# Turned feed-forward rows copied out of PSUM first and split from the copy, the last product of w_down in banks of its own, and the last row divided at column 352

## Chip, cores and metric

The kernel runs on one core of a Trainium2 chip, as one launch. The metric is the device time of the launch in microseconds (us), smaller is better. Engines are named as in the profile: PE is TensorE (matrix products and transposes), PEld its weight loads, DVE is VectorE, ACT is ScalarE, POOL is GpSimd, SP is SyncE, which issues most DMAs. The granted TensorE clock of the profiled execution is 0.999 of full speed.

## What is computed

The reference is one encoder layer on 512 tokens of width 1024 in float32. Two mixers (a state-space scan and a gated MLP) are merged and added to the residual stream `h`, a cross-attention to 256 memory tokens follows, then a gated feed-forward block, then a last normalization. The change lies in the last two:

```python
def rms_norm(x, g):
    xf = x.astype(jnp.float32)
    y = xf * lax.rsqrt(jnp.mean(xf * xf, axis=-1, keepdims=True) + EPS)
    return (y * g.astype(jnp.float32)).astype(x.dtype)

def swiglu(hn, w_gate, w_up, w_down):
    return (jax.nn.silu(hn @ w_gate) * (hn @ w_up)) @ w_down
...
        h = h + memory_cross_attention(rms_norm(h, xattn_norm_g[i]), memn,
                                       w_q[i], w_k[i], w_v[i], w_xo[i])
        h = h + swiglu(rms_norm(h, ffn_norm_g[i]), w_gate[i], w_up[i], w_down[i])
    return rms_norm(h, final_norm_g)
```

`w_gate` and `w_up` are 1024 by 2816, `w_down` is 2816 by 1024.

## The kernel before

**Numbers in two halves.** Every large product keeps float32 accuracy by splitting each operand into a high half (`hi`, the value rounded by ScalarE to the type that TensorE multiplies, L85) and a low half (`lo`, the value minus `hi`, a DVE subtraction, L86). A product is three matmuls, hi by hi, hi by lo and lo by hi (`mm3`, L374). Weights come by DMA into `wraw` (three buffers) and are split into `whi` and `wlo` (three buffers each) some steps ahead of their use; a fixed list, `plan`, gives the order of loads and splits, and `next_w` moves along it.

**Rows.** The 512 tokens are four rows of 128 tokens, numbered 0 to 3. The residual stream `h` holds each row as 128 partitions by 1024 columns, and its column halves are `HALF[0]` and `HALF[1]`.

**Turned rows.** The feed-forward products need the normalized rows with features on the partitions. Once a row of `h` is final, its sum of squares is taken (L500), GpSimd takes the root (L511), DVE scales the row into `xs` (two halves, L526), and `to_feat` turns it: for each half `q`, four transposes on TensorE write one PSUM buffer `ptr` (L534), then `split` makes `fn_hi` (ScalarE) and `fn_lo` (DVE) from it, and ScalarE copies it unsplit into `full` (L540). `ptr` comes from the pool `paux`, which has three buffers. `full` is needed since the gate and up products run in Strassen form: sums of quarters of the activation are made from it (L1720 to L1730). Rows 0 and 1 are turned between the blocks of the attention's output product, in written order; rows 2 and 3 among the first feed-forward products (`pf`, `px`, `pv`), where the scheduler places them.

**The product with w_down.** It is a Strassen product of seven (`DOWN`, in the order 1, 5, 2, 6, 3, 7, 4), each of six chunks of rows of `w_down`; chunk 5 is half as deep as the others. A product covers two rows of tokens and 512 columns. Its partial results lie in pairs of PSUM banks `dx`, `dv` and `dq` and are added into `h` by DVE (`onto_h`, L1934). Products 6, 7 and 4 accumulate on top of each other in `dx`, and `h` takes what is there after 6 and after 7. Product 4 is the last: it is needed only for rows 2 and 3, second half. Its first three chunks run for both rows, the last three (`HELD`) first for row 2 and then, in two pieces of 256 columns in `dv`, for row 3, seeded with the sum of `h` and the bank (L1902).

**The end.** Each row's first finished half is multiplied by the gain `g_o` early and kept in `hg`, a part of the tile `rest` (L1874). When a row's second half is done, its sum of squares gives the factor `r` (L1880, L1881), `hg` is scaled by ScalarE (L1918), the other half by DVE (L1920, L1926, L1928), and both are stored. For row 3 SyncE stores the part of `hg` and ScalarE's queue the part of `h`. From the last chunk's products on, the order of DVE and ACT is the written one (`in_order`).

Of the kernel before, what the change touches and what calls it, by code (L numbers as in the profile page):

```python
# [11 lines left out]
AF = mybir.ActivationFunctionType  # L12
ALU = mybir.AluOpType
# [4 lines left out]
P = 128  # L18
D = 1024
T = 512  # L20
NT = T // P
# [31 lines left out]
def hybrid_layer_kernel(  # L53
# [8 lines left out]
    nc = tc.nc  # L62
    x, mem, out = x[0], mem[0], out[0]
# [13 lines left out]
    def bank(name):  # L77
        return pm.tile([P, 512], F32, tag="mm", name=name)

    def aux(name, shape=(P, 512)):  # L80
        return pa.tile(list(shape), F32, tag="aux", name=name)

    def split(dst_hi, dst_lo, src):

        hi = nc.scalar.copy(dst_hi, src)  # L85
        lo = nc.vector.tensor_tensor(dst_lo, src, dst_hi.bitcast(F32), ALU.subtract)  # L86
        if pinned[0]:
            in_order(hi)
            in_order(lo)
        return hi  # L90
# [3 lines left out]
    in_order = tc.keep_in_program_order  # L94
# [165 lines left out]
    DOWN, CHUNKS = (1, 5, 2, 6, 3, 7, 4), 6  # L260
# [110 lines left out]
    def mm3(ps, a, b, start, stop, free=False, turn=False):  # L371

        for i, (x, y) in enumerate(((0, 0), (0, 1), (1, 0))):
            m = nc.tensor.matmul(ps, a[x], b[y], start=start and i == 0, stop=stop and i == 2, skip_group_check=free)  # L374
            if turn:
                in_order(m)
# [90 lines left out]
    def tick(us=5.2):  # L467

        side["now"] += us / 5.2
        run_due()  # L470
        side["credit"] = min(side["credit"] + us * side["rate"], us)
        while side["credit"] > 0.0 and side["gen"] is not None:
            try:
                used = next(side["gen"])
            except StopIteration:
                side["gen"] = None
                return
            if used is None:
                side["credit"] = 0.0
                return  # L480
            side["credit"] -= used
# [32 lines left out]
    HALF = (slice(0, 512), slice(512, 1024))  # L514
# [10 lines left out]
        for i in range(2):  # L525
            nc.vector.scalar_tensor_tensor(dst[:, HALF[i]], src[:, HALF[i]], r, g[:, HALF[i]], ALU.mult, ALU.mult)  # L526

    def to_feat(src, hi, lo, tsl, full=None, skip=None, part=(0, 1), turned=False):

        for q in part:  # L530
            ps = aux("ptr", (P, 4, P))
            for j in range(4):
                k = 4 * q + j
                m = nc.tensor.transpose(ps[:, j, :], src[:, k * P:(k + 1) * P], ident)  # L534
                if turned:
                    in_order(m)
            if q != skip:
                split(hi[:, 4 * q:4 * q + 4, tsl], lo[:, 4 * q:4 * q + 4, tsl], ps)
            if full is not None:
                nc.scalar.copy(full[:, 4 * q:4 * q + 4, tsl], ps)  # L540

    xsp = [None]
# [11 lines left out]
    def slot(tag, shape, dt, name, place=NEAR):  # L554
        n = math.prod(shape[1:])
        t = sp.tile([P, KD * T + ROOM[tag]], dt, tag=tag, name=name)[:, place[tag]:place[tag] + n]
        return t.rearrange("p (a b c) -> p a b c", a=shape[1], b=shape[2]) if len(shape) == 4 else (
            t.rearrange("p (a b) -> p a b", a=shape[1]))

    def token_slot(name, place=NEAR):  # L560
        return tuple(slot(tag, (P, KD, T), F32R, name, place) for tag in "BC")
# [374 lines left out]
    turned = set()  # L936
# [263 lines left out]
    for h in range(H):  # L1200
        ps = bank("psv")
# [56 lines left out]
    def unit_bank(name):  # L1258
        return bank(name).rearrange("p (j t) -> p j t", j=2)
# [15 lines left out]
    part = slot("A", (P, KD, T), F32, "part")  # L1275
# [133 lines left out]
    h = slot("A", (P, NT, D), F32, "h")  # L1409
# [202 lines left out]
    fn_hi, fn_lo = token_slot("fn", AWAY)  # L1612
# [3 lines left out]
    ps = {t: bank(f"pt{t}") for t in range(NT)}  # L1616
# [32 lines left out]
    full = fp.tile([P, KD, T], F32, tag="full", name="full", bufs=1)  # L1649


    scaled = {}
# [3 lines left out]
        rms_scale(h[:, t, :], g_f, xs, ss)  # L1656

    def turn_row(t, turned=False):
        to_feat(scaled.pop(t), fn_hi, fn_lo, slice(t * P, (t + 1) * P), full, turned=turned)

    fin = add_evac(1, 1, scale_row)
    held, ps = [], {}
# [91 lines left out]
    ps = [bank("pf0"), bank("pf1")]  # L1754
# [51 lines left out]
    def rows_product(ps, q, c, ops_, ts, cs, start, stop, turn=False):  # L1806
        hi, lo = ops_
        a = made[q, c // 2]
        for t in ts:
            tsl = slice(t * P, (t + 1) * P)  # L1810
            for k in range(hi.shape[1]):
                kk = 2 * (c % 2) + k
                mm3(ps[t], (a[0][:, kk, tsl], a[1][:, kk, tsl]), (hi[:, k, cs], lo[:, k, cs]),
                    start and k == 0, stop and k == hi.shape[1] - 1, True, turn)
        tick(1.35 * len(ts))
# [6 lines left out]
    for i, u in enumerate(UNITS):  # L1822
        final = i == len(UNITS) - 1
        x, v = begun
        q = unit_bank("pq")
# [12 lines left out]
        else:  # L1838
            dx = [bank(f"dx{t}") for t in range(2)]
# [20 lines left out]

    g_o = gain(final_norm_g, "g_o")
    hg = rest[0][:, 4:8, :]
    msq = fp.tile([P, NT + 2], F32, name="msq", bufs=1)

    def mean_sq(dst, ss, base):
# [2 lines left out]
    early, HELD = {}, 3  # L1868

    def first_half(t, half):  # L1870

        early[t] = half
        sum_sq(hss[:, 2, t, half:half + 1], h[:, t, HALF[half]])
        nc.vector.tensor_tensor(hg[:, t, :], h[:, t, HALF[half]], g_o[:, HALF[half]], ALU.mult)  # L1874
        nc.vector.tensor_scalar(msq[:, t:t + 1], hss[:, 2, t, half:half + 1], 1.0 / D, EPS, ALU.mult, ALU.add)

    def inv_root(t, ss):
        r = np_.tile([P, 1], F32, tag="r", name="r", bufs=2)
        ms = np_.tile([P, 1], F32, tag="ms", name="ms", bufs=2)
        root = nc.scalar.activation(ms, ss, AF.Sqrt, bias=msq[:, t:t + 1], scale=1.0 / D)  # L1880
        inv = nc.vector.reciprocal(r, ms)  # L1881
        if pinned[0]:
            in_order(root)
            in_order(inv)
        return r
# [11 lines left out]
    last = [dv[i][:, 0:256] for i in range(2)]  # L1897
    last_cols = [slice(512 + 256 * i, 768 + 256 * i) for i in range(2)]

    def seed_last(ps):  # L1900
        for i in range(2):
            in_order(nc.vector.tensor_tensor(last[i], h[:, NT - 1, last_cols[i]], ps[:, 256 * i:256 * i + 256], ALU.add))  # L1902

    def finish_last(i):
        ss = np_.tile([P, 2], F32, tag="ss", name="ss", bufs=2)
        sum_sq(ss[:, 0:1], last[i])
        in_order(nc.vector.tensor_tensor(h[:, NT - 1, last_cols[i]], last[i], g_o[:, last_cols[i]], ALU.mult))
        if i == 0:
            mean_sq(msq[:, NT:NT + 1], ss[:, 0:1], msq[:, NT - 1:NT])
        else:  # L1910
            write(NT - 1, inv_root(NT, ss[:, 0:1]))

    stores = []

    def write(t, r):
        rows = out[t * P:(t + 1) * P]
        cs, hs = HALF[early[t]], HALF[1 - early[t]]
        scaled = nc.scalar.activation(hg[:, t, :], hg[:, t, :], AF.Copy, scale=r)  # L1918
        if t < 2:
            nc.vector.scalar_tensor_tensor(h[:, t, hs], h[:, t, hs], r, g_o[:, hs], ALU.mult, ALU.mult)  # L1920
            stores.extend([(rows[:, cs], hg[:, t, :]), (rows[:, hs], h[:, t, hs])])
            return
        in_order(scaled)
        nc.sync.dma_start(rows[:, cs], hg[:, t, :])
        if t == NT - 1:
            in_order(nc.vector.tensor_scalar(h[:, t, hs], h[:, t, hs], r, None, ALU.mult))  # L1926
        else:
            in_order(nc.vector.scalar_tensor_tensor(h[:, t, hs], h[:, t, hs], r, g_o[:, hs], ALU.mult, ALU.mult))  # L1928
        (nc.scalar if t == NT - 1 else nc.sync).dma_start(rows[:, hs], h[:, t, hs])

    def onto_h(ps, t0, half, op):
        for t in range(2):
            hs = h[:, t0 + t, HALF[half]]
            nc.vector.tensor_tensor(hs, hs, ps[t], op)  # L1934

    dq = [bank("dq0"), aux("dq1")]
# [7 lines left out]
    for t in range(2):  # L1944
        first_half(t, 1)
# [5 lines left out]
        finish(t)  # L1951
    down_product(dx, 7, False)
    onto_h(dx, 2, 0, ALU.subtract)
    for t in range(2, 4):
        first_half(t, 0)

    held = []
    for c in range(CHUNKS):
        ops_ = next_w(w_down, 4, c)
        if c == CHUNKS - 1 - LOADS:  # L1960
            for dst, src in stores:
                in_order(nc.sync.dma_start(dst, src))
        if c < CHUNKS - HELD:
            rows_product(dx, 4, c, ops_, (0, 1), slice(0, 512), False, c == CHUNKS - HELD - 1)
        else:
            held.append((c, ops_))
    seed_last(dx[1])
    for c, ops_ in held:
        rows_product(dx, 4, c, ops_, (0,), slice(0, 512), False, c == CHUNKS - 1, True)
    pinned[0] = True  # L1970
    in_order(nc.vector.tensor_tensor(h[:, 2, HALF[1]], h[:, 2, HALF[1]], dx[0], ALU.add))
    finish(2)
    for i in range(2):
        for c, ops_ in held:
# [36 lines left out]
```

## Time and profile before

| | us |
|---|---|
| median of 3 runs | 864.61 (863.97 to 865.8) |
| profiled execution, its own time | 865.88 |
| its span | 864.1 |
| PE busy | 855.3 (99%) |
| DVE busy | 662.2 (77%) |
| ACT busy | 465.9 (54%) |
| POOL busy | 88.4 (10%) |

The span is the part of the profiled execution between its first and last instruction. A line of the groups or of the timeline names the source line, the engine, the operation, what it writes and reads with shapes, its count, and in brackets how long its engine was idle ahead of it and what ended that idle time. All moments are microseconds from the start of the span.

### The profile page before, as it was taken

The page shows a single profiled execution, that of the slowest core. Times are in us where ns is not written, and L with a number is a line of the kernel's source. Part 1 is how long each engine was busy: PE and PEld are TensorE (multiplying, and loading weights), DVE is VectorE, ACT ScalarE, POOL GpSimd, SP SyncE. Part 2 cuts the span into 40 slices and gives each one's busy share as a digit, 9 for nine tenths or more (in the row PEclk, how much of TensorE's full clock was granted, in tenths as well). Part 3 has the DMA queues.
Part 4 walks back from the last instruction along what each step waited for, and adds up shares of the span by engine and source line. Part 5 has one row for each costly group of instructions (what it writes and reads, how often), then busy time and mean ns, then how long its engine had stood idle before and what let it go on. Part 6 is the DMA issues. An engine that isn't in the chain of part 4 may idle for free.

```text
span 864.1 us, 14763 instructions
## 1 busy us (share of the span) xinstructions
PE 855.3 (99%) x5776; PEld 766.1 (89%) x5776; DVE 662.2 (77%) x1077; ACT 465.9 (54%) x698; POOL 88.4 (10%) x119
## 2 busy tenths in 40 slices
PE   9999999999999999999999999999999999999997
PEld 7888888888889988899899887999999999988886
DVE  7698999899646867678758655867877768899875
ACT  6734863244445544457557544645545454655674
POOL 0002211211021110010010001001211111000000
PEclk9999999999999999999999999999999999999999
DMA  8759576988574798635696455557899898366664
GB/s 271 191 166 315 100 216 157 234 201 208 139 220 157 248 308 267 218 112 197 214 273 169 130 160 134 146 167 182 207 241 231 213 229 219 96 192 205 199 187 155
DMA packets 116041, 170.09 MB, mean 197 GB/s; under 512 B 9458, under 2 KB 80642, under 8 KB 115843
## 3 DMA queue, kind: packets, MB, share of 16 engines
q1 hardware_dynamic: 95618, 140.07, 49.3%
q0 software_dynamic: 20064, 28.55, 20.4%
q8 instruction: 45, 0.74, 0.3%
q10 hardware_dynamic: 288, 0.52, 0.2%
q14 instruction: 26, 0.21, 0.1%
HBM read 160.23 MB, written 48.73 MB: 242 GB/s over the span
## 4 chain that ended last, share of the span: by engine, by line
PE 96%; DVE 1%; DMA 1%; issue 0%; ACT 0%; POOL 0%; SPq 0%; POOLq 0%; ACTq 0%
PE pf L374 27%; PE pt L374 15%; PE px L1250 13%; PE dx L374 7%; PE pq L1250 6%; PE dq L374 3%; PE pv L1250 3%; PE bx L1250 3%; PE qx L1250 3%; PE dv L374 2%; PE pz L958 2%; PE qv L1250 1%; PE po L374 1%; PE psc L374 1%; PE py L1014 1%; PE qq L1250 1%
## 5 line engine op out<-in xcount | busy, mean ns | idle before, releaser
L85 ACT CAST whi<-wraw 128x1024 fp32r<-128x1024 f32 x141 | 145.3, 1030 | 163.9 <-PE pf L374 56.3
L86 DVE TENSOR_TENSOR wlo<-wraw,whi 128x1024 fp32r<-128x1024 f32 x141 | 168.4, 1196 | 59.7 <-ACT whi L85 58.9
L374 PE MATMUL pf<-xn,whi 128*128 128x512 f32 x448 | 139.6, 392 | 0.0
L374 PEld LDWEIGHTS pf<-xn,whi 128*128 128x128 f32 x448 | 83.5, 188 | 16.7
L374 PE MATMUL pf<-xn,wlo 128*128 128x512 f32 x224 | 87.8, 392 | 0.0
L1250 PE MATMUL px<-fn,whi 128*128 128x256 f32 x480 | 83.4, 277 | 0.0
L1250 PEld LDWEIGHTS px<-fn,whi 128*128 128x128 f32 x480 | 72.5, 188 | 0.2
L86 DVE TENSOR_TENSOR wlo<-b,whi 128x1024 fp32r<-128x1024 f32 x40 | 49.0, 1224 | 26.0 <-ACT whi L85 26.0
L85 ACT CAST whi<-b 128x1024 fp32r<-128x1024 f32 x40 | 42.2, 1054 | 48.7 <-PE px L1250 27.8
L1250 PE MATMUL px<-fn,wlo 128*128 128x256 f32 x240 | 66.4, 277 | 0.0
L1250 PE MATMUL pq<-s,whi 128*128 128x256 f32 x320 | 55.0, 276 | 0.0
L374 PE MATMUL dx<-whi,s 128*128 128x512 f32 x166 | 52.2, 391 | 0.4 <-DVE h L1934 0.4
L86 DVE TENSOR_TENSOR wlo<-t,whi 128x1024 fp32r<-128x1024 f32 x30 | 36.7, 1225 | 18.4 <-ACT whi L85 18.4
L85 ACT CAST whi<-t 128x1024 fp32r<-128x1024 f32 x30 | 31.6, 1054 | 34.2 <-PE pv L1250 11.4
L374 PEld LDWEIGHTS pf<-xn,wlo 128*128 128x128 f32 x224 | 42.0, 188 | 8.9 <-issue 0.2
L1250 PEld LDWEIGHTS pq<-s,whi 128*128 128x128 f32 x320 | 48.2, 188 | 0.0
L1250 PEld LDWEIGHTS px<-fn,wlo 128*128 128x128 f32 x240 | 45.1, 188 | 0.0
L1250 PE MATMUL pq<-s,wlo 128*128 128x256 f32 x160 | 44.2, 276 | 0.0
L374 PE MATMUL pt<-whi,xn 128*128 128x512 f32 x128 | 43.1, 403 | 0.0
L374 PEld LDWEIGHTS dx<-whi,s 128*128 128x128 f32 x166 | 31.1, 188 | 7.4 <-ACT whi L85 0.8
L374 PE MATMUL dx<-wlo,s 128*128 128x512 f32 x83 | 32.1, 389 | 0.0
L289 POOL DMA_DIRECT2D dsum<-in_w_down_dram x12 | 13.2, 1104 | 173.0 <-DMA dsum<-in_w_down_dram 169.3
(457 smaller groups left out, 2223.8 us busy)
## 6 DMA issues: line engine op xcount, KB each, us to landing
wraw<-in_w_in_dram SPq DMA_DIRECT2D x34, 512.0 KB, 4.7
dsum<-in_w_down_dram SPq DMA_DIRECT2D x20, 512.0 KB, 5.5
wraw<-dsum SPq DMA_DIRECT2D x20, 512.0 KB, 3.9
b<-in_w_gate_dram SPq DMA_DIRECT2D x15, 512.0 KB, 6.7
b<-in_w_up_dram SPq DMA_DIRECT2D x15, 512.0 KB, 5.7
wraw<-in_w_down_dram SPq DMA_DIRECT2D x15, 512.0 KB, 4.9
dsum<-in_w_down_dram POOLq DMA_DIRECT2D x10, 512.0 KB, 7.9
dsum<-dsum POOLq DMA_DIRECT2D x10, 512.0 KB, 8.0
```

The costliest lines, as they stand in the source:

```text
L85: hi = nc.scalar.copy(dst_hi, src)
L86: lo = nc.vector.tensor_tensor(dst_lo, src, dst_hi.bitcast(F32), ALU.subtract)
L289: plan[j + step][1].append((0, lambda d=dst, x=more: nc.gpsimd.dma_start(d, x, accum_op=ALU.add)))
L374: m = nc.tensor.matmul(ps, a[x], b[y], start=start and i == 0, stop=stop and i == 2, skip_group_check=free)
L958: nc.tensor.matmul(ps[:, g, :], wt[:, g, :], u[:, o * GO + g, :], start=True, stop=True)
L1014: in_order(nc.tensor.matmul(ps[64 * j:64 * j + 64, :, :, h, :].rearrange("p q d c -> p d q c"), a, b, start=k == ks[0], stop=k == ks[2], t ...
L1250: nc.tensor.matmul(ps[:, j, :], a[x], b[y], start=start and j == k == i == 0, stop=k == 3 and i == 2, skip_group_check=True)
```

## The change

It has three parts.

First, `to_feat` gets a flag `copied`, set for the feed-forward rows alone. With it ScalarE first copies the PSUM buffer into `full`, and `split` then makes `fn_hi` and `fn_lo` from `full`, which lies in SBUF. `ptr` is read by that copy only.

Second, product 4 no longer accumulates on 6 and 7 in `dx`. It starts afresh in the pair `dq`, and what `dx` held is added to the second half of rows 2 and 3 by two more DVE sums (`onto_h(dx, 2, 1, ALU.add)`).

Third, the slots of `hg` are handed out in another order (`HG`), so that row 3's first half and the free quarter behind it make one stretch of 1024 columns, `last_row`. The row's last products are written there instead of into `h`. ScalarE scales and SyncE stores columns 0 to 351, DVE scales and ScalarE's queue stores columns 352 to 1023 (`write_last`). The slot behind row 3's is the one in which row 0's half was kept.

```diff
-    def to_feat(src, hi, lo, tsl, full=None, skip=None, part=(0, 1), turned=False):
+    def to_feat(src, hi, lo, tsl, full=None, skip=None, part=(0, 1), turned=False, copied=False):
...
+            src_ = ps
+            if full is not None and copied:
+                src_ = full[:, 4 * q:4 * q + 4, tsl]
+                nc.scalar.copy(src_, ps)
             if q != skip:
-                split(hi[:, 4 * q:4 * q + 4, tsl], lo[:, 4 * q:4 * q + 4, tsl], ps)
-            if full is not None:
+                split(hi[:, 4 * q:4 * q + 4, tsl], lo[:, 4 * q:4 * q + 4, tsl], src_)
+            if full is not None and not copied:
                 nc.scalar.copy(full[:, 4 * q:4 * q + 4, tsl], ps)
...
-        to_feat(scaled.pop(t), fn_hi, fn_lo, slice(t * P, (t + 1) * P), full, turned=turned)
+        to_feat(scaled.pop(t), fn_hi, fn_lo, slice(t * P, (t + 1) * P), full, turned=turned, copied=True)
...
+    HG = (2, 3, 0, 1)
+    last_row = hg[:, 1:3, :].rearrange("p a c -> p (a c)")
+    CUT = 352
...
-        in_order(nc.vector.tensor_tensor(h[:, NT - 1, last_cols[i]], last[i], g_o[:, last_cols[i]], ALU.mult))
+        in_order(nc.vector.tensor_tensor(last_row[:, last_cols[i]], last[i], g_o[:, last_cols[i]], ALU.mult))
         if i == 0:
             mean_sq(msq[:, NT:NT + 1], ss[:, 0:1], msq[:, NT - 1:NT])
         else:
-            write(NT - 1, inv_root(NT, ss[:, 0:1]))
+            write_last(inv_root(NT, ss[:, 0:1]))
...
+    def write_last(r):
+        rows = out[(NT - 1) * P:NT * P]
+        x, y = last_row[:, 0:CUT], last_row[:, CUT:D]
+        in_order(nc.scalar.activation(x, x, AF.Copy, scale=r))
+        in_order(nc.vector.tensor_scalar(y, y, r, None, ALU.mult))
+        nc.sync.dma_start(rows[:, 0:CUT], x)
+        nc.scalar.dma_start(rows[:, CUT:D], y)
...
     onto_h(dx, 2, 0, ALU.subtract)
+    onto_h(dx, 2, 1, ALU.add)
...
-            rows_product(dx, 4, c, ops_, (0, 1), slice(0, 512), False, c == CHUNKS - HELD - 1)
+            rows_product(dq, 4, c, ops_, (0, 1), slice(0, 512), c == 0, c == CHUNKS - HELD - 1)
...
-    seed_last(dx[1])
+    seed_last(dq[1])
     for c, ops_ in held:
-        rows_product(dx, 4, c, ops_, (0,), slice(0, 512), False, c == CHUNKS - 1, True)
+        rows_product(dq, 4, c, ops_, (0,), slice(0, 512), False, c == CHUNKS - 1, True)
     pinned[0] = True
-    in_order(nc.vector.tensor_tensor(h[:, 2, HALF[1]], h[:, 2, HALF[1]], dx[0], ALU.add))
+    in_order(nc.vector.tensor_tensor(h[:, 2, HALF[1]], h[:, 2, HALF[1]], dq[0], ALU.add))
```

The order of instructions moves at three places. ScalarE at the turned rows 0 and 1 (`ptr` is the PSUM buffer of the transposes, `whi` the high half of weights, `b` and `wraw` their sources) ran before:

```order
L85 CAST fn<-ptr 128x4x128 x2
L85 CAST whi<-b_5488 128x1024
L540 COPY full<-ptr 128x4x128
L85 CAST whi<-wraw 128x1024
L540 COPY full<-ptr 128x4x128
L85 CAST fn<-ptr 128x4x128 x2
L540 COPY full<-ptr 128x4x128 x2
```

and the same place on ScalarE in the changed kernel has:

```order
L540 COPY full<-ptr 128x4x128 x2
L85 CAST fn<-full 128x4x128 x2
L85 CAST whi<-b_5488 128x1024
L85 CAST whi<-wraw 128x1024
L540 COPY full<-ptr 128x4x128 x2
L85 CAST fn<-full 128x4x128 x2
```

Each row's copies now stand ahead of its casts, and both weight casts stand between row 0 and row 1. On TensorE, not shown here, the transposes of row 2 stand five matmuls of `px` later than before, and row 3's second four transposes stand two matmuls of `pf` behind its first four, where before sixteen lay between.

VectorE at the start of the last product (`dx_8076` and `dx_8077` are the banks of rows 2 and 3, `s_...` pieces of the left operand) ran before:

```order
L86 TENSOR_TENSOR s_8921<-a_low,s_8921 128x1024
L1934 TENSOR_TENSOR h<-h,dx_8076 128x512
L86 TENSOR_TENSOR wlo<-wraw,whi 128x1024
L1934 TENSOR_TENSOR h<-h,dx_8077 128x512
L1874 TENSOR_TENSOR rest<-h,g_o 128x512
L86 TENSOR_TENSOR wlo<-wraw,whi 128x1024
L86 TENSOR_TENSOR s_8960<-rest,s_8960 128x512
```

and on VectorE in the changed kernel:

```order
L86 TENSOR_TENSOR s_8923<-a_low,s_8923 128x1024
L1947 TENSOR_TENSOR h<-h,dx_8076 128x512 x2
L86 TENSOR_TENSOR wlo<-wraw,whi 128x1024
L1947 TENSOR_TENSOR h<-h,dx_8077 128x512 x2
L1881 TENSOR_TENSOR rest<-h,g_o 128x512
L86 TENSOR_TENSOR wlo<-wraw,whi 128x1024
L86 TENSOR_TENSOR s_8962<-rest,s_8962 128x512
```

Each bank's sum into `h` is doubled, ahead of the low halves of the weights of chunk 1 and of chunk 2.

TensorE where product 7 ends and product 4 begins (`s_8837` is product 7's left operand, `s_8878` product 4's) ran before:

```order
L374 MATMUL dx_8077<-wlo,s_8837 128x512
L374 MATMUL dx_8077<-whi,s_8837 128x512
L374 MATMUL dx_8076<-whi,s_8878 128x512
L374 MATMUL dx_8076<-wlo,s_8878 128x512
L374 MATMUL dx_8076<-whi,s_8878 128x512 x2
```

and on TensorE in the changed kernel:

```order
L374 MATMUL dx_8077<-wlo,s_8837 128x512
L374 MATMUL dx_8077<-whi,s_8837 128x512
L374 MATMUL dq_8217<-whi,s_8878 128x512
L374 MATMUL dq_8218<-whi,s_8878 128x512
L374 MATMUL dq_8217<-wlo,s_8878 128x512
L374 MATMUL dq_8217<-whi,s_8878 128x512 x2
```

Product 4 now writes the pair `dq`, and takes both rows of tokens chunk by chunk, where before it took row 2's part of two chunks ahead of row 3's.

More of the change, by code (lines that the diff above doesn't have):

```diff
@@ L1873, in first_half @@
         sum_sq(hss[:, 2, t, half:half + 1], h[:, t, HALF[half]])
-        nc.vector.tensor_tensor(hg[:, t, :], h[:, t, HALF[half]], g_o[:, HALF[half]], ALU.mult)
+        nc.vector.tensor_tensor(hg[:, HG[t], :], h[:, t, HALF[half]], g_o[:, HALF[half]], ALU.mult)
         nc.vector.tensor_scalar(msq[:, t:t + 1], hss[:, 2, t, half:half + 1], 1.0 / D, EPS, ALU.mult, ALU.add)
@@ L1917, in write @@
         cs, hs = HALF[early[t]], HALF[1 - early[t]]
-        scaled = nc.scalar.activation(hg[:, t, :], hg[:, t, :], AF.Copy, scale=r)
+        hgt = hg[:, HG[t], :]
+        scaled = nc.scalar.activation(hgt, hgt, AF.Copy, scale=r)
         if t < 2:
             nc.vector.scalar_tensor_tensor(h[:, t, hs], h[:, t, hs], r, g_o[:, hs], ALU.mult, ALU.mult)
-            stores.extend([(rows[:, cs], hg[:, t, :]), (rows[:, hs], h[:, t, hs])])
+            stores.extend([(rows[:, cs], hgt), (rows[:, hs], h[:, t, hs])])
             return
         in_order(scaled)
[L1924 to L1929, printed above, removed]
+        nc.sync.dma_start(rows[:, cs], hgt)
+        in_order(nc.vector.scalar_tensor_tensor(h[:, t, hs], h[:, t, hs], r, g_o[:, hs], ALU.mult, ALU.mult))
+        nc.sync.dma_start(rows[:, hs], h[:, t, hs])
+    def write_last(r):
[5 more added lines that the diff above has]
+        nc.scalar.dma_start(rows[:, CUT:D], y)
     def onto_h(ps, t0, half, op):
```

## The prediction

> **What bounds the kernel now.** I read the page's table of busy times and its chain that ended last first, then TensorE's waits from 524 us to the end, then the timeline at the two places that these name, and last the end.
>
> ```profile
> PE 855.3 (99%) x5776; PEld 766.1 (89%) x5776; DVE 662.2 (77%) x1077; ACT 465.9 (54%) x698; POOL 88.4 (10%) x119
> PE 96%; DVE 1%; DMA 1%; issue 0%; ACT 0%; POOL 0%; SPq 0%; POOLq 0%; ACTq 0%
> ```
>
> TensorE is busy for 99% of the span and carries 96% of the chain (which starts at the last instruction and goes back), so an edit pays only where it closes a hole in TensorE's work or shortens the stretch behind its last matmul. The waits of PE (matmuls) show all holes of the part that the change touches:
>
> ```profile
> PE ptr L534 <- ACT full L540: 1.2, 1, 1.2
> PE dx L374 <- DVE h L1934: 0.4, 1, 0.4
> ```
>
> There are two, of 1.2 and 0.4 us, and each is aimed at by one edit. The first is among the turned rows (timeline of all engines, start and duration in us, then the instruction):
>
> ```profile
> 528.06 1.06 ACT L85 CAST fn<-ptr 128x512 fp32r<-128x512 f32 x2
> 529.00 1.06 ACT L85 CAST whi<-b 128x1024 fp32r<-128x1024 f32 x1
> 529.26 1.42 DVE L526 SCALAR_TENSOR_TENSOR xs<-h,r,g_f 128x512 f32<-128x512 f32 x2 [0.73 <-POOL r L511]
> 530.07 0.66 PE L534 MATMUL ptr<-ident,xs 128*128 128x128 f32 x4
> 531.31 0.59 ACT L540 COPY full<-ptr 128x512 f32<-128x512 f32 x1 [1.25 <-DVE fn L86]
> 531.95 0.66 PE L534 MATMUL ptr<-ident,xs 128*128 128x128 f32 x4 [1.23 <-ACT full L540]
> ```
>
> Row 0's two halves and row 1's first half hold the three PSUM buffers of the pool `paux`. Row 1's second half needs the first of them back, and gets it only when the copy to `full` of 531.31 is done, at 531.90. That copy was itself kept back by a DVE subtraction, as the 1.25 us of idle ahead of it say.
>
> **Edit 1, copy first.** With the copy in the place of the hi cast, row 0's two copies run at about 528.06 to 529.12 (the copy takes 0.59 us, as the cast does), and from then on nobody else reads the buffers. Row 1's second half then waits only for its scaled row: the two DVE scalings end at 529.26 + 1.42 = 530.68. The first half's transposes began 0.06 us behind their scaling (529.26 + 0.75, the mean of L526, is 530.01; they began at 530.07), so the second four start at 530.74 instead of 531.95: TensorE gains 1.21 us. Both ends: 1.27 if they follow at once, 1.1 if the step from scaling to transposes takes 0.17.
>
> What it costs is a step more in front of the halves `fn`: copy, then cast, then subtraction, each from SBUF. Groups of ACT and DVE (count | busy us, mean ns | idle before), with a cast of the same size from SBUF, `mg_hi`:
>
> ```profile
> L85 ACT CAST fn<-ptr 128x512 fp32r<-128x512 f32 x8 | 4.5, 591 | 1.7 <-PE ptr L534 1.6
> L526 DVE SCALAR_TENSOR_TENSOR xs<-h,r,g_f 128x512 f32<-128x512 f32 x8 | 5.7, 750 | 4.4 <-POOL r L511 4.4
> L85 ACT CAST mg_hi<-mg 128x512 fp32r<-128x512 f32 x8 | 4.8, 620 | 4.6 <-DVE mg L1396 4.6
> ```
>
> The source in SBUF costs ScalarE 29 ns a cast, eight times, and ScalarE has gaps there (1.7 us ahead of these casts alone): nothing on TensorE's path. The subtraction, whose other source lies in SBUF already, I leave at its 0.69 us, from the rows below. The delay must be held against what TensorE wants next. These rows give it:
>
> ```profile
> 534.06 1.28 DVE L86 TENSOR_TENSOR fn<-ptr,fn 128x512 fp32r<-128x512 f32 x2
> 537.92 0.40 PE L374 MATMUL pf<-fn,s 128*128 128x256 f32 x2
> 538.02 1.42 DVE L526 SCALAR_TENSOR_TENSOR xs<-h,r,g_f 128x512 f32<-128x512 f32 x2 [0.73 <-POOL r L511]
> 541.10 0.60 PE L534 MATMUL ptr<-ident,xs 128*128 128x128 f32 x4
> 545.29 0.60 PE L534 MATMUL ptr<-ident,xs 128*128 128x128 f32 x4
> 548.85 0.69 DVE L86 TENSOR_TENSOR fn<-ptr,fn 128x512 fp32r<-128x512 f32 x1 [0.63 <-ACT fn L85]
> 550.99 0.40 PE L1256 MATMUL idle<-fn 128*128 128x512 f32 x1
> ```
>
> Row 1: ScalarE now runs row 0's copies and casts to 530.2, the two weight casts (1.06 each) to 532.3, row 1's copies to 533.4 and casts to 534.5; the second subtraction ends at about 535.4, as it does now (534.06 + 1.28 = 535.34). The first matmul of `pf` comes 1.21 earlier, at 536.7, so 1.3 us are to spare. Row 2's sum into `h` follows that subtraction on DVE and stays where it is, and so does its scaled row, ready at 538.02 + 1.42 = 539.44; its transposes (541.10) come 1.2 earlier with TensorE and move five matmuls back in its order, 0.6 us, so they start near 540.5 and find it ready. Row 3's transposes start about 1.1 earlier (544.2); its copies stand behind a weight cast (1.06) and a copy to `pv` as long as their own (0.59), and even if these begin only then, the copies end at 547.0, the casts at 548.1 and the last subtraction at 548.8. TensorE wants it at 550.99 - 1.21 = 549.8: 1.0 to spare. Were either cover gone, TensorE would give back what is late, one for one, up to 1.2 for a further pair of ACT steps. SyncE's and GpSimd's orders hold the same steps as before; loads there are released by DVE and TensorE, so they move with them.
>
> Whether a lead of 1.2 us lasts to the end is read from ScalarE's waits between 551 and 842 us, a stretch in which PE has no wait in the list above:
>
> ```profile
> ACT whi L85 <- PE px L1250: 34.2, 25, 1.8
> ```
>
> The weight casts there wait for TensorE to give buffers back, not TensorE for them. They will come earlier with it, and I keep the lead in full.
>
> **Edit 2, last product in `dq`.** The timeline at its start, of all engines:
>
> ```profile
> 842.27 0.69 DVE L1934 TENSOR_TENSOR h<-h,dx 128x512 f32<-128x512 f32 x1
> 842.30 0.39 PE L374 MATMUL dx<-whi,s 128*128 128x512 f32 x1
> 842.88 1.22 DVE L86 TENSOR_TENSOR wlo<-wraw,whi 128x1024 fp32r<-128x1024 f32 x1
> 843.11 0.47 PE L374 MATMUL dx<-whi,s 128*128 128x512 f32 x1 [0.42 <-DVE h L1934]
> 843.41 0.39 PE L374 MATMUL dx<-wlo,s 128*128 128x512 f32 x1
> 845.21 1.22 DVE L86 TENSOR_TENSOR wlo<-wraw,whi 128x1024 fp32r<-128x1024 f32 x1
> 854.79 0.28 PE L374 MATMUL dv<-whi,s 128*128 128x256 f32 x1
> ```
>
> The matmul of 843.11 would write `dx[0]` while DVE still reads it. From 843.11 to 854.79 there are 51 matmuls (36 of the first three chunks, 15 of row 2's rest), 0.229 us each. Without the wait the next two would have come at 842.53 and 842.76; they came at 843.11 and 843.41. So 0.65 us are gained by the second; 0.42, the wait as listed, is the lower end. `dq` was last read after product 3, a whole product earlier, so nothing takes the wait's place there.
>
> The price is two more DVE sums (`dx` into the second half of rows 2 and 3), at 0.60 us each by the starts 842.27 and 842.88. They stand ahead of weight halves. By the times of before, with the product starting at 842.53 and 12 matmuls a chunk (2.75 us): the low half of chunk 1 would start at 843.48 and end at 844.70, while TensorE, which now does both rows' first matmul ahead of it, wants it at 845.28 + 0.46 = 845.74; that of chunk 2 (two sums and a gain product, 0.60 each, in front) starts 1.2 later than now, at 846.41, ends at 847.64 and is wanted at 848.49; that of chunk 3, behind two token pieces and another gain product (1.5 in all), ends near 850.5 and is wanted at 851.0. The loads of chunks 4 and 5 are issued when those subtractions are done, so 0.6 and 1.2 later, and still land ahead of their casts (3 to 4 us to landing). The cost is nothing, covered by 0.5 us at the thinnest; without the cover at most 0.6 for a sum.
>
> **Edit 3, the end.** ACT's and DVE's last steps, the two stores, and DMA by stretch (time, PE, PEld, DVE, ACT and POOL busy, clock, DMA share, GB/s):
>
> ```profile
> 859.61 0.72 ACT L1918 ACTIVATE rest<-rest,r 128x512 f32<-128x512 f32 x1 [0.23 <-DVE r L1881]
> 859.61 0.49 DVE L1926 TENSOR_SCALAR h<-h,r 128x512 f32<-128x512 f32 x1
> 860.13 0.35 ACTq L1929 DMA_DIRECT2D out_dram<-h  x1
> 860.36 0.33 SPq L1924 DMA_DIRECT2D out_dram<-rest  x1
> 860.90:862.50 1.60, 0.00 (x0) 0.00 (x0) 0.00 (x0) 0.00 (x0) 0.00 (x0) 1.00 0.85 328
> L500 ACT ACTIVATE sq<-h 128x512 f32<-128x512 f32 x3 | 1.9, 632 | 7.2 <-DVE h L1440 7.2
> L500 ACT ACTIVATE sq<-dv 128x256 f32<-128x256 f32 x2 | 0.8, 375 | 0.4 <-PE dv L374 0.4
> out_dram<-h SPq DMA_DIRECT2D x3, 256.0 KB, 3.0
> out_dram<-rest SPq DMA_DIRECT2D x4, 256.0 KB, 2.5
> ```
>
> ScalarE's 352 columns take 0.72 - 160 x 1.0 ns = 0.56 us (1.0 ns a column from 632 and 375), so its store is issued at 860.20 instead of 860.36. VectorE's 672 take between 0.49 (the row for 512) and 0.64 (in proportion); I take 0.59, so its store is issued near 860.23 instead of 860.13. 328 GB/s for 1.6 us are 525 KB, both stores: they share one stream without a hole, so its end follows the first issue, which comes 0.07 later. I take +0.1; the ends are -0.13 (the later of both issues counts, 860.36 to 860.23) and +0.5 (as far as the landing of equal stores, 2.5 and 3.0, lies apart).
>
> The Trainium skill (VectorE: DVE Perf Modes, the section Mode 2x_2P) says that a one-source fp32 operation in SBUF delivers two elements a cycle; at its 0.96 GHz the 160 columns more would be an estimate of 0.08 us, 0.57 in all, and the sum would be 0.02 better. No row here shows the slope.
>
> The Trainium skill (DMA: Bandwidth & Descriptors, How a descriptor splits into AXI transactions) speaks against the cut: a piece that doesn't start at a multiple of 256 bytes fetches from the boundary below it. The second piece starts at byte 1,408, so 132 beats move a row instead of 128; as an estimate the 1.6 us grow by 0.05 and the sum is that much worse. No run so far shows it.
>
> **Sum.** -1.21 - 0.65 + 0.10 = -1.76 us, between -2.0 and -1.0 by the ends. The profiled execution took 865.88 us, 1.8 of it outside its span of 864.1; it would become 864.12. The median of the runs, 864.61, is 1.27 below it, and the sum applies to it too: 862.85.
>
> **Rivals.** (1) The lead of 1.21 us is not kept: the turned halves come late after all, because ScalarE's order puts two weight casts ahead of row 1's copies. For it speaks that every half now has two ACT steps; against it the 1.3 and 1.0 us to spare. It would leave -0.55: 864.05. (2) The two sums hold weight halves back in the last product. Against it are margins of 0.5 to 1.0; for it, that these rest on a DVE that runs without a gap. At 0.6 lost it gives -1.15: 863.45. (3) Slower: the last row's products (L1907, now L1914) are written into the quarter of `rest` from which row 0's half is stored, so DVE waits for that store, and behind it in DVE's queue are the mean square and the last root.
>
> ```profile
> 846.83 0.43 SPq L1962 DMA_DIRECT2D out_dram<-rest  x1
> 858.17 0.42 DVE L1907 TENSOR_TENSOR h<-dv,g_o 128x256 f32<-128x256 f32 x1 [0.36 <-ACT sq L500]
> ```
>
> The store is issued at 846.83 and takes about 2.5; the product starts at 858.17, or 856.3 with the gain. From a landing at 856.3 on each us costs one: at 860 the end is 3.7 - 1.76 = 1.9 later, 866.5. Seven us of cover speak against it.
>
> **How the numbers follow.** A measurement of this kernel can tell about 0.2% from no change: 1.73 us, so the forecast lies on that bound. I give the forecast 0.75, (1) 0.12, (2) 0.08, (3) 0.05. Of the forecast's 0.75 some 0.48 lie beyond 1.73 us (its ends reach from -1.0 to -2.0, and three runs of before lie 1.8 apart) and 0.27 within; (1) and (2) are within. Faster 0.48, same 0.47, slower 0.05. The range runs from the best end (-2.0) with a run's scatter of 0.7, 861.9, to just past (1), 864.5.
>
> **What would show it.** Right: no wait of PE on `full`, four transposes near 530.8, `pf` near 536.7, matmuls of `dq` right behind those of `dx`, PE's last matmul 1.9 us earlier, first packets of the last stores some 0.1 us later after the last root than now. Wrong: PE waiting on `fn` (rival 1), on `wlo` or `whi` behind the new sums (rival 2), DVE at L1914 on a DMA (rival 3), or a last transfer much longer than 1.6 us.

## The result, and the profile after

The changed kernel took 864.21 us, median of 13 runs (863.06 to 865.15); the kernel before, beside it, 865.60 in 13 runs (863.97 to 868.01). The ratio is 0.9984, with an interval of [0.9976, 0.9992], so 1.4 us less, between 0.7 and 2.1. In a later series it was 864.37 against 865.23, ratio 0.9988 [0.9979, 0.9997]. The change is a gain, and a gain inside the 0.2% (1.73 us) that the prediction set as its bound. The forecast was 862.85. A ratio with its interval comes from all runs of both kernels and is not exactly the quotient of the two medians: in the later series the medians alone differ by 0.86 us, the ratio says 1.0.

The profiled execution took 865.15 us with a span of 863.4, where the one of before took 865.88 and 864.1. That is 0.7 less, half of what the medians say: the profiled execution of the changed kernel was the slowest of its 13 runs, and the turned rows below show what was late in it. First the busy times of the page, and the whole list of PE's waits from 524 us to the end of the changed kernel:

```profile
PE 855.7 (99%) x5776; PEld 766.2 (89%) x5776; DVE 662.6 (77%) x1079; ACT 465.5 (54%) x698; POOL 88.5 (10%) x119
PE ptr L534 <- DVE xs L526: 0.2, 1, 0.2
```

A hole is a time in which TensorE has nothing to do because it waits. Both old holes, 1.2 us at the transposes and 0.4 at product 4, are gone, and there is no wait on `fn`, `whi` or `wlo`. What is left is 0.2 us on the scaled row itself. The turned rows, in the timeline of the changed kernel:

```profile
526.21 1.41 DVE L526 SCALAR_TENSOR_TENSOR xs<-h,r,g_f 128x512 f32<-128x512 f32 x2 [2.87 <-POOL r L511]
527.01 1.32 PE L534 MATMUL ptr<-ident,xs 128*128 128x128 f32 x8 [0.16 <-DVE xs L526]
530.14 1.41 DVE L526 SCALAR_TENSOR_TENSOR xs<-h,r,g_f 128x512 f32<-128x512 f32 x2 [0.73 <-POOL r L511]
530.95 1.38 PE L534 MATMUL ptr<-ident,xs 128*128 128x128 f32 x8
532.82 1.08 ACT L540 COPY full<-ptr 128x512 f32<-128x512 f32 x2
534.95 1.28 DVE L86 TENSOR_TENSOR fn<-full,fn 128x512 fp32r<-128x512 f32 x2
537.63 0.40 PE L374 MATMUL pf<-fn,s 128*128 128x256 f32 x2
547.63 1.29 DVE L86 TENSOR_TENSOR fn<-full,fn 128x512 fp32r<-128x512 f32 x2 [0.88 <-ACT fn L85]
550.65 0.39 PE L1260 MATMUL idle<-fn 128*128 128x512 f32 x1
```

Row 1's eight transposes now stand in one run (530.95, x8), where before four came at 530.07 and four at 531.95. But `pf` begins at 537.63, only 0.29 us ahead of the 537.92 of before: in this execution row 1 was scaled by 531.55 (530.14 + 1.41), 0.87 us later than the 530.68 of before. Counted from the scaled row, `pf` comes 6.08 us behind, where before it came 7.24 behind: the edit gave its 1.16 us, and a late row took most of it back. The chain that ended last names what was late (start, duration, what), first of before, then of the changed kernel:

```profile
514.99 7.80 DMA t<-in_w_gate_dram
523.37 1.32 POOL t L192
524.69 0.61 POOL r L511
525.32 1.41 DVE xs L526 x2
```

```profile
515.27 8.40 DMA t<-in_w_gate_dram
524.25 1.32 POOL t L192
526.21 0.76 DVE xs L526
```

Row 0's root (`r`, L511) stands on GpSimd's queue behind the issue of a DMA (L192), and that issue waits until the load of `t` has landed. The load began 0.28 us later in the second execution and took 8.40 us instead of 7.80, for the same bytes. No part of the change touches it. Row 1 inherits the delay: its scaling starts 3.93 or 3.94 us behind row 0's in both (529.26 - 525.32, 530.14 - 526.21).

Product 4 and the end, first the last root in the timeline of before, then the changed kernel's timeline, and the transfer by stretch (time, PE, PEld, DVE, ACT and POOL busy, clock, DMA share, GB/s):

```profile
859.43 0.15 DVE L1881 RECIPROCAL r<-ms 128x1 f32<-128x1 f32 x1
```

```profile
842.17 0.39 PE L374 MATMUL dx<-whi,s 128*128 128x512 f32 x1
842.40 0.62 PE L374 MATMUL dq<-whi,s 128*128 128x512 f32 x2
853.96 0.28 PE L374 MATMUL dv<-whi,s 128*128 128x256 f32 x1
857.34 0.42 DVE L1914 TENSOR_TENSOR rest<-dv,g_o 128x256 f32<-128x256 f32 x1 [0.36 <-ACT sq L500]
858.60 0.15 DVE L1888 RECIPROCAL r<-ms 128x1 f32<-128x1 f32 x1
858.78 0.59 ACT L1939 ACTIVATE rest<-rest,r 128x352 f32<-128x352 f32 x1 [0.23 <-DVE r L1888]
858.78 0.57 DVE L1940 TENSOR_SCALAR rest<-rest,r 128x672 f32<-128x672 f32 x1
859.38 0.38 ACTq L1942 DMA_DIRECT2D out_dram<-rest  x1
859.39 0.33 SPq L1941 DMA_DIRECT2D out_dram<-rest  x1
860.20:861.80 1.60, 0.00 (x0) 0.00 (x0) 0.00 (x0) 0.00 (x0) 0.00 (x0) 0.50 0.87 328
```

The products in `dq` follow the last of `dx` with no hole, and from there to the first matmul of `dv` it is 11.79 us, where before it was 12.49 (842.30 to 854.79): 0.70 gained. From the end of the last root to the end of the span it is 4.62 us (858.747 to 863.368), before 4.53 (859.579 to 864.112; a page rounds spans to a tenth, the trace holds them to a thousandth): 0.09 lost. So 0.74 us = 0.29 + 0.70 - 0.09 - 0.16, the last for what goes between `pf` and product 4 (304.54 us, before 304.38).

### The profile page after: what moved, and what is told of

Same layout as the page of the kernel before. It is cut to its first block, busy times and chain, and to the rows that moved or that the text cites. A ratio compares the mean times of both kernels' runs of the same rounds, so it can differ in the third digit from the quotient of the medians.

```text
span 863.4 us, 14762 instructions
## 1 busy us (share of the span) xinstructions
PE 855.7 (99%) x5776; PEld 766.2 (89%) x5776; DVE 662.6 (77%) x1079; ACT 465.5 (54%) x698; POOL 88.5 (10%) x119
## 4 chain that ended last, share of the span: by engine, by line
PE 91%; DMA 4%; DVE 3%; ACT 1%; issue 1%; POOL 0%; SPq 0%; POOLq 0%; ACTq 0%; DVEq 0%
PE pf L374 23%; PE pt L374 14%; PE px L1254 13%; PE pq L1254 6%; PE dx L374 5%; PE dq L374 5%; PE pv L1254 3%; PE bx L1254 3%; PE qx L1254 3%; PE dv L374 2%; DMA wraw<-in_w_out_dram 2%; PE pz L962 2%; PE qv L1254 1%; PE po L374 1%; PE psc L374 1%; PE py L1018 1%
## 5 line engine op out<-in xcount | busy, mean ns | idle before, releaser
L374 PE MATMUL dx<-whi,s 128*128 128x512 f32 x132 | 41.4, 390 | 0.0
L374 PE MATMUL dq<-whi,s 128*128 128x512 f32 x122 | 38.1, 389 | 0.0
L500 ACT ACTIVATE sq<-h 128x512 f32<-128x512 f32 x23 | 14.5, 630 | 30.8 <-DVE h L1444 24.6
```

The source lines that it names most:

```text
L500: act = nc.scalar.activation(sq[:, :src.shape[-1]], src, AF.Square, bias=bias, accum_out=dst)
```

## Experiments

Eight kernels were run, four and then four more. My theory: edit 1 gives about 1.16 us where the scaled row sets the pace, edit 2 gives 0.7, edit 3 costs 0.1. The rival that the first profile suggested: the lead of edit 1 reaches the end only in part.

**Each edit alone.** The first has the `copied` lines alone (kernel before with):

```diff
+            if full is not None and copied:
+                src_ = full[:, 4 * q:4 * q + 4, tsl]
+                nc.scalar.copy(src_, ps)
...
```

> The kernel before with the copy ahead of the split alone. My theory: the hole of 1.2 us at row 1's second four transposes goes, since only the scaled row holds them; measured from the end of row 1's scaling on DVE to the first matmul of pf the time falls from 7.2 us (before) to about 6.1, as in the changed kernel, and the product 4 wait of 0.4 us stays. Total -1.2 us (ratio 0.9986). Rival (lead not kept): the hole goes, but fn comes late or the chain in front (DMA for t, GpSimd's root) moves back by as much, so that product 4 starts within 0.3 us of before; total 0 to -0.4 (ratio 0.9996 to 1).

Measured: 864.58 us (863.95 to 865.47, 11 runs) against 865.44 (864.21 to 868.78, 33 runs), ratio 0.9983 [0.9974, 0.9993]; the medians alone differ by 0.86 us. PE's only wait from 524 us on, and the timeline:

```profile
PE dx L374 <- DVE h L1938: 0.4, 1, 0.4
522.48 1.33 POOL L192 DMA_DIRECT2D t<-in_w_gate_dram  x1 [12.18 <-DMA t<-in_w_gate_dram]
526.40 1.04 PE L534 MATMUL ptr<-ident,xs 128*128 128x128 f32 x8
528.38 1.42 DVE L526 SCALAR_TENSOR_TENSOR xs<-h,r,g_f 128x512 f32<-128x512 f32 x2 [0.73 <-POOL r L511]
536.40 0.40 PE L374 MATMUL pf<-fn,s 128*128 128x256 f32 x2
```

Here the issue on GpSimd came at 522.48, 1.8 us earlier than in the first profile of the changed kernel, and row 1 was scaled by 529.80. With 6.08 behind it `pf` could have come at 535.88; it came at 536.40, with no wait of PE: now PE's own list sets the moment, 10.00 us behind row 0's transposes. The expected 6.1 was missed: the stretch from row 1's scaling to `pf` measures 6.60 here. So the edit's worth has a second bound that I had not reckoned with.

The second moves product 4 alone:

```diff
+    onto_h(dx, 2, 1, ALU.add)
...
-            rows_product(dx, 4, c, ops_, (0, 1), slice(0, 512), False, c == CHUNKS - HELD - 1)
+            rows_product(dq, 4, c, ops_, (0, 1), slice(0, 512), c == 0, c == CHUNKS - HELD - 1)
...
```

> The kernel before with the last product in dq alone. My theory: no wait of PE between products 7 and 4; from the last matmul of product 7 in dx to the first of dv the time falls by 0.65 to 0.7 us (12.49 before: 842.30 to 854.79), low halves of chunks 1 to 3 come 0.6 to 1.2 us later and nobody waits for them; the hole of 1.2 us at the turned rows stays. Total -0.65 (ratio 0.9992). Rival (sums hold the weight halves back): PE or PEld waits on wlo or whi in product 4, and the stretch falls by 0.3 or less or grows.

Measured: 864.33 us, ratio 0.9987 [0.9978, 0.9996], so 0.3 to 1.9 us less. PE's only wait from 524 us on, and the timeline of product 4:

```profile
PE ptr L534 <- ACT full L540: 1.0, 1, 1.0
842.17 0.39 PE L374 MATMUL dx<-whi,s 128*128 128x512 f32 x1
842.40 0.62 PE L374 MATMUL dq<-whi,s 128*128 128x512 f32 x2
853.96 0.28 PE L374 MATMUL dv<-whi,s 128*128 128x256 f32 x1
```

The stretch is 11.79 us, 0.70 less than before; the hole at the transposes stays, the one at product 4 is gone, and no wait on a weight half has come in its place. The two sums cost TensorE nothing.

The third has `write_last` with its cut at column 352, and the other two edits undone.

```diff
+        x, y = last_row[:, 0:CUT], last_row[:, CUT:D]
...
+        nc.sync.dma_start(rows[:, 0:CUT], x)
+        nc.scalar.dma_start(rows[:, CUT:D], y)
```

> The kernel before with the last row divided at column 352 alone. My theory: one stream carries both stores, so the end follows the first issue; from the end of the last root on DVE to the end of the span it takes 4.5 us before and 4.6 with the cut. Total +0.1 (ratio 1.0001), no difference that timing can show. Rival (the later of both issues counts): 4.5 falls to 4.3 or 4.4, total -0.13.

Measured: 865.05 us, ratio 0.9995 [0.9982, 1.0009]: the time alone tells nothing. The timeline of the end:

```profile
858.51 0.15 DVE L1888 RECIPROCAL r<-ms 128x1 f32<-128x1 f32 x1
859.30 0.38 ACTq L1942 DMA_DIRECT2D out_dram<-rest  x1
```

From the end of the last root (858.665) to the end of the span (863.282) it is 4.62 us, as in the changed kernel. The rival's 4.3 to 4.4 is out.

**The row's moment.** The fourth kernel takes the root of rows 0 and 1 off GpSimd's queue, in the changed kernel:

```diff
+        nc.vector.tensor_scalar(ms, ss[:, 0:1], 1.0 / D, EPS, ALU.mult, ALU.add)
+        nc.scalar.activation(ms, ss[:, 1:2], AF.Sqrt, bias=ms, scale=1.0 / D)
+        nc.vector.reciprocal(r, ms)
...
```

> The changed kernel with the root of rows 0 and 1 taken by ScalarE and DVE instead of GpSimd, whose queue holds it behind a DMA that waits for the load of t. My theory: in the changed kernel the turned rows start when that DMA lets GpSimd go (row 0's scaling began at 526.2, and at 525.3 in the profile of before), so without GpSimd row 0's scaling begins near 524.6 whatever the DMA does, TensorE no longer waits for xs, and pf begins 6.5 us or less after row 0's last product; product 4 starts 0.5 to 1.2 us earlier than in the changed kernel. Total -0.3 to -1.2 beside the changed kernel, about -2 to -2.5 beside before (ratio 0.9973). Rival: the table load and two more steps on ScalarE (1.3 us and 0.3 each) stand in front of row 0 and give the time back; no difference to the changed kernel.

Measured: 863.94 us (862.99 to 864.51), ratio 0.9981 [0.9972, 0.9989]. Its timeline:

```profile
523.46 1.33 POOL L192 DMA_DIRECT2D t<-in_w_gate_dram  x1 [12.92 <-DMA t<-in_w_gate_dram]
526.49 1.04 PE L534 MATMUL ptr<-ident,xs 128*128 128x128 f32 x8
528.03 1.42 DVE L1669 SCALAR_TENSOR_TENSOR xs<-h,r,g_f 128x512 f32<-128x512 f32 x2
536.49 0.40 PE L374 MATMUL pf<-fn,s 128*128 128x256 f32 x2
```

The issue came as late as in before (523.46 against 523.37), yet row 1 was scaled by 529.45, 1.23 us earlier than there. It helps up to PE's list and no further: `pf` again 10.00 behind row 0's transposes. So of the 2 to 2.5 us that were expected beside before, 1.5 came by the medians.

The same three lines in the kernel before put the question the other way round: with an early row, is there anything left for the copy to gain?

> The kernel before, with only the root of rows 0 and 1 taken from GpSimd's queue (there it stands behind an issue that waits for a load) to ScalarE and VectorE. Row 1's scaling should then end at about 529.5 us, not 530.7. Theory (the copy behind the split costs only what the row's lateness leaves over PE's own list, first feed-forward product at row 1 plus 7.24 us): first product at 536.7, where PE's own list gives 536.4 to 536.5, so the copy-first edit would be worth only 0.2 us here; whole time some 0.7 to 1.1 us under before (ratio about 0.999), and its runs spread less than those of before. Rival (the copy behind the split costs PE 1.16 us whenever the row comes): first product at 537.6 or later, time as before within 0.2 us.

Measured: 864.45 us (864.04 to 865.15, 11 runs) against 865.23 (864.08 to 869.06, 30 runs), ratio 0.9985 [0.9974, 0.9995]. PE's waits (all of them from 524 us on) and the timeline:

```profile
PE dx L374 <- DVE h L1943: 0.4, 1, 0.4
526.67 1.04 PE L534 MATMUL ptr<-ident,xs 128*128 128x128 f32 x8
528.21 1.42 DVE L1665 SCALAR_TENSOR_TENSOR xs<-h,r,g_f 128x512 f32<-128x512 f32 x2
536.87 0.40 PE L374 MATMUL pf<-fn,s 128*128 128x256 f32 x2
```

With the split still ahead of the copy, the wait on `full` has left the list, and `pf` begins at 536.87, within 0.2 us of what PE's list allows (526.67 + 10.00); the rest is a wait of 0.23 us on `full` that the weight loads (PEld) of row 1's second four transposes show. The rival's 537.6 is out. A row that comes 1 us earlier (scaled by 529.63 instead of 530.68) closes nearly the same hole as the copy does, so the two gains don't add.

The changed kernel itself ran once more:

> The changed kernel once more, unchanged, for a second profile beside the others. Theory (row 1's scaling comes when a load lands, differently in each execution; behind it 6.08 us to the first feed-forward product, but never before 536.4, PE's own list): the product starts at the later of 536.4 and row 1's end plus 6.08. Ratio to before 0.9984, between 0.9976 and 0.9992. Rival (a fixed gain at every moment): product at 536.7 whenever row 1 ends as in before, 530.7, and 7.24 less 1.16 behind it also where row 1 ends before 530.3.

Measured: 864.37 us (863.43 to 865.59), ratio 0.9988 [0.9979, 0.9997]. Its timeline:

```profile
526.05 1.04 PE L534 MATMUL ptr<-ident,xs 128*128 128x128 f32 x8
528.54 1.42 DVE L526 SCALAR_TENSOR_TENSOR xs<-h,r,g_f 128x512 f32<-128x512 f32 x2 [0.73 <-POOL r L511]
536.06 0.40 PE L374 MATMUL pf<-fn,s 128*128 128x256 f32 x2
```

Nothing was changed, and yet row 1 was scaled 1.59 us earlier than in the first profile of this kernel and `pf` began 1.57 us earlier; the span is 1.52 us shorter (861.846 against 863.368). VectorE's last sum into row 0 of `h` (L1444) came 0.65 us earlier too (520.80 against 521.45), so part of this stems from what ran ahead; the rest is the load, whose landing differs between executions of one kernel. Of the 1.57 us nearly all reaches the end.

My floor of 536.4 was wrong as a moment: `pf` came at 536.06. It is right as a distance. All ten profiles agree with one rule: `pf` begins at the later of (row 0's transposes + 10.00) and (end of row 1's scaling + 6.08 with the copy first, + 7.24 with the split first). The 7.24 is taken from before, the 6.08 from the first profile of the changed kernel and the 10.00 from the copy alone. Of the other seven, three test the 7.24 and four the 10.00. No second profile lies on the 6.08: the changed kernel's second shows only that it is not above 6.11.

| profile | row 0's transposes | row 1 scaled | `pf` by the rule | `pf` measured |
|---|---|---|---|---|
| before (split first) | 526.42 | 530.68 | 537.92 | 537.92 |
| product 4 alone (split first) | 526.58 | 530.58 | 537.82 | 537.81 |
| last row alone (split first) | 525.89 | 529.71 | 536.95 | 536.94 |
| before, root moved (split first) | 526.67 | 529.63 | 536.87 | 536.87 |
| changed (copy first) | 527.01 | 531.55 | 537.63 | 537.63 |
| changed, again | 526.05 | 529.96 | 536.05 | 536.06 |
| copy alone | 526.40 | 529.80 | 536.40 | 536.40 |
| three stores (below) | 526.78 | 530.44 | 536.78 | 536.79 |
| changed, root moved | 526.49 | 529.45 | 536.49 | 536.49 |
| both (below) | 526.32 | 529.29 | 536.32 | 536.32 |

By the rule, putting the copy first is worth 1.16, 1.16 and 1.06 us in the three profiles with the split first and the root on GpSimd, and 1.16, 1.15, 0.64 and 0.90 in the four with the copy first and the root on GpSimd (worked out against the same moments with 7.24): 1.03 on the mean. With the root moved it is 0.2. These are estimates by the rule; no execution can be run both ways.

**The end.** A kernel that lets the first store go earlier, in the changed kernel (`y0` is the first 256 of VectorE's columns, `y1` the other 416):

```diff
+        MID = CUT + 256
...
+        in_order(nc.vector.tensor_scalar(y0, y0, r, None, ALU.mult))
+        in_order(nc.vector.tensor_scalar(y1, y1, r, None, ALU.mult))
+        nc.scalar.dma_start(rows[:, CUT:MID], y0)
...
+        nc.scalar.dma_start(rows[:, MID:D], y1)
```

> The changed kernel, with the last row's 672 VectorE columns done and stored in two pieces: the first 256 (131 KB) go as soon as they are scaled, then 416, so that three stores end the kernel. Theory (the stores run as one stream that begins a fixed time after the first issue, and the end follows that stream): the first issue comes some 0.2 us earlier, last root to end of span falls from 4.6 to 4.35 to 4.5 us, about 0.15 us beside the changed kernel. Rival (the end follows the last issue, or the third store's own overhead): 4.6 to 4.8 us. The whole time can tell neither from the changed kernel; the stretch in the trace decides.

Measured: 863.77 us (863.17 to 864.39), ratio 0.9979 [0.9970, 0.9988]. The timeline of its end:

```profile
857.70 0.15 DVE L1888 RECIPROCAL r<-ms 128x1 f32<-128x1 f32 x1
857.88 0.35 DVE L1942 TENSOR_SCALAR rest<-rest,r 128x256 f32<-128x256 f32 x1
858.15 0.43 DVE L1943 TENSOR_SCALAR rest<-rest,r 128x416 f32<-128x416 f32 x1
858.27 0.35 ACTq L1944 DMA_DIRECT2D out_dram<-rest  x1
858.50 0.33 SPq L1945 DMA_DIRECT2D out_dram<-rest  x1
858.71 0.39 ACTq L1946 DMA_DIRECT2D out_dram<-rest  x1
```

The span ended at 862.226: 4.38 us behind the root, where the four profiles with two stores cut at 352 have 4.61 to 4.62 and the four with equal halves 4.53 to 4.55 (mean 4.54). From the first issue to the end of the span it is 3.95 to 4.00 us in all ten profiles, whether there are two stores or three, cut evenly or not; from the last issue it is 3.75 to 3.77 with equal halves, 3.97 with the cut and 3.51 with three stores. The theory holds: the end follows the first issue. The drop of the whole time by 0.6 beside the changed kernel (864.37) is more than the 0.24 that the trace shows, and within the scatter of these runs.

Last, this and the moved root together:

> The changed kernel with both: the root of rows 0 and 1 off GpSimd's queue and the last row in three stores. If the two do not touch each other: first feed-forward product at 536.5, last root to end of span 4.35 to 4.5 us, whole time 863.7 to 863.9, ratio to before 0.998 (lowest of all). Rival (the early row only trades one wait for another, or the third store costs what it saves): as the changed kernel, 0.9984.

Measured: 863.53 us (862.83 to 864.71, 9 runs), ratio to before 0.9978 [0.9969, 0.9988], the lowest median of all, 0.84 below the changed kernel in the same series. The intervals of the two overlap. In its profile `pf` comes at 536.32 and the end 4.37 us behind the last root, as expected of both parts; the time lies a little under the expected 863.7 to 863.9.

## Why the prediction was right, and where it was off

**Edit 1, right in mechanism, off in what bounds it.** The hole went, the cover held: row 1's low halves were ready at 536.23 (534.95 + 1.28) and used at 537.63, so 1.4 us to spare where 1.3 were forecast; row 3's at 548.92 and used at 550.65, so 1.7 where 1.0 were forecast. Row 2's transposes moved back by 0.7 in PE's order (3.89 us behind the first `pf`, before 3.18), forecast 0.6. The step that failed is "the second four start at 530.74 instead of 531.95: TensorE gains 1.21 us". It took row 1's moment, 530.68, from one profile as if it were fixed. In seven profiles that moment lies between 529.71 and 531.55, and when it comes early PE's own list stands in the way after part of the gain. By the rule above the term is 1.16 at a late row, 0.64 at an early one, 1.03 on the mean. So two of the prediction's signs came otherwise in the first profile: the second four transposes at 531.70 instead of near 530.8, `pf` at 537.63 instead of 536.7. PE's first product in `dv` came 0.83 us earlier than before in that profile and 2.35 earlier in the second, where 1.9 was forecast for the last.

**The lead kept in full.** Nearly: from `pf` to the last matmul of `dx` ahead of product 4 it is 304.36 to 304.46 us in the four profiles with the split first and 304.48 to 304.59 in the six with the copy first, 0.12 more on the mean. The traces put the loss near the start: TensorE's first 150 instructions from `pf` on, among which the transposes of rows 2 and 3 have moved, take 17.44 or 17.45 us with the copy first and 17.28 to 17.31 with the split first. Why the moved order costs this, no run shows.

**Edit 2, right.** 0.70 measured in all six profiles that have it (11.78 or 11.79 us against 12.49), 0.65 forecast, and nothing took the hole's place.

**Edit 3, right.** 0.08 lost (4.62 against 4.54), 0.10 forecast, and by the step that was named: both stores leave together, at 859.38, and the end follows the first issue, which comes 0.63 us behind the root where before it came 0.55 behind. The first packets of the last stores come 1.48 us behind the root, before 1.42. The stream still moves 328 GB/s over 1.6 us. ScalarE's 352 columns took 0.59 us (forecast 0.56) and VectorE's 672 took 0.57 (forecast 0.59).

The estimate from the Trainium skill (VectorE: DVE Perf Modes, Mode 2x_2P), two fp32 elements a cycle, was 0.57 for the 672 columns: the trace agrees, and with 0.35 us for 256, 0.43 for 416 and 0.57 for 672 the slope is 0.53 ns a column. The estimate from the Trainium skill (DMA: Bandwidth & Descriptors, How a descriptor splits into AXI transactions), 0.05 us more for rows cut at byte 1,408, was not seen: from the first packet of the last stores to the end of the last one the traces have 1.51 us in the four profiles with that cut and 1.51 or 1.52 in the four with equal halves. The packets of one row took about 171 ns together with the cut and 169 without.

**The sum.** By the pieces: -1.03 + 0.12 - 0.70 + 0.08 = -1.5 us; by the ratios of the two comparisons -1.4 and -1.0; forecast -1.76. Of the 1.36 us between the forecast of 862.85 and the 864.21 measured, only 0.37 is the change (-1.39 by the medians). The other 0.99 is the base: the forecast was laid on 864.61, the median of three runs of before, and thirteen runs have 865.60. The base and the first term were off in the same direction, and the measured time lies 0.3 us inside the upper end of the range: that it lies inside owes more to the width of the range than to the sum. On which side of the 0.2% the gain would lie, the prediction left nearly even (0.48 to 0.47), so that it came out inside says little for it.

**The rivals.** The first (lead not kept, 864.05; its sum of -0.55 gives 864.06) is nearer to the number that came out than the forecast is, but not by its mechanism: PE waits nowhere on `fn`, and the edit alone gave 0.9983, an interval that ends below the rival's 0.9996. The second (sums hold weight halves) is out, with no wait on `wlo` or `whi` in the changed kernel or with product 4 alone. The third (L1914 behind the store of row 0) is out: L1914 waits 0.36 us for ScalarE's squares, as before.

**Still open.** Runs of before reach 868 to 869 us, and so does the last row alone (869.07); the kernels with the copy first stay under 865.6, product 4 alone under 865.4 and before with the moved root under 865.2. A late row could lengthen a run like this, but no profile shows an execution of that length, and product 4 alone has the same late row, so the cause stays open.

## What to carry to other kernels

A hole behind a wait is worth what the next bound leaves of it: before pricing an edit, work out when the engine's own list would bring the next matmul if nothing waited, and where the operand's moment comes from. If that moment hangs on a load's landing, it differs from one execution to the next, and two edits that close the same hole don't add. At the end of a kernel whose last stores run as one stream, as here, get the first store's issue forward.

## What the runs showed of the hardware

GpSimd's queue passes a load's lateness on to work that has nothing to do with the load. In all seven profiles with the root there, row 0's scaling began 1.96 or 1.97 us after the issue on GpSimd (L192), which itself came at 522.39 to 524.24; in the three with the root on ScalarE and VectorE the scaling began 1.18, 0.69 and 1.28 us after that issue, and no longer followed it.

A third store cost less at the end than the earlier start of the first gained. In the two profiles that have it, first to last packet of the last stores took 1.59 us instead of 1.51, but the first packet came 1.27 us behind the root instead of 1.48. The span ended 3.95 or 3.96 us after the first issue, where it is 3.98 to 4.00 with two stores.
